# Hybrid decoder trunk: two-tensor work moved from POOL to VectorE, gates split from branch products, a new order of the mixers

## The chip, the cores and the metric

One core of one Trainium2 chip runs the whole program. The time is that of one execution on the device in microseconds, the median of several runs. TensorE (PE) multiplies, VectorE (DVE), ScalarE (ACT) and GpSimd (POOL) work elementwise, SyncE (SP) issues the DMAs. The stationary operand of a matmul comes in by a weight load (PEld), which overlaps the matmul before it.

## What is computed

A decoder trunk of two layers over 512 tokens of width 1024, in float32. In each layer four causal token mixers read one normed input, each is projected, gated and summed; then a feed-forward follows:

```
h = RMSNorm(x)
[u_nsa | u_sb | u_gla | u_fox | gate_logits] = h @ W_in
y_i = mixer_i(u_i)                                       # (512, 512) each
x = x + (sum_i sigmoid(gate_logits_i + b_gate_i) * (y_i @ W_branch_i)) @ W_out
x = x + relu(RMSNorm(x) @ W_ff1)^2 @ W_ff2
```

The mixers are native sparse attention (nsa: 8 heads, of which compressed, selected and sliding-window results are each multiplied by a sigmoid gate and summed), stick-breaking attention (sb), gated linear attention in chunks (gla) and forgetting attention (fox).

## The kernel before, in words

Everything is held transposed: a tile is 128 features x 512 tokens. To keep float32's accuracy at the faster matmul type, each factor is split in a high and a low half (`hh`, `hl` for the input, `wh` and the ring buffer `wr` for the weights, `yh`, `yl` for a mixer's output), and a product takes three matmuls. Weights come as one stream of chunks of 128x1024, 512 KB each, in the very order in which they are used. `chunk` (L305) loads one into a ring of three buffers, ScalarE makes its high half (L315) and VectorE the low half (L316). `mtile` (L319) multiplies a chunk with the input in 24 matmuls of 512 columns; `scaled` (L414) reads the product out of PSUM.

The mixers are cut into pieces, and the list `MIXERS` (L1496) writes out by hand in which order their instructions are issued. `sb_att.1.3` is step 3 of pair of heads 1 of stick-breaking attention, `nsa.2.5` step 5 of pair 2 of nsa, `nsa_cmp.0.1` its compressed part, `gla.0.4` step 4 of pair 0 of gla. The scheduler that builds the program follows the list as a priority and fixes each engine's order at build time by a clock of its own. The same list gives the order of the weight stream (`weight_stream`, L1515).

The places that matter here:
- `branch(n, qt)` (L763) first makes two gates (two `mtile`s, bias, sigmoid; tiles `gt`, two buffers), then multiplies `y_n` by a chunk of `W_branch` (24 matmuls), times the gate on VectorE (L794), added into `mixed` on POOL (L796).
- `nsa(pi)` (L1208): for each head and branch, scores (`pass1`, `pass2`), row maxima, probabilities, `pv`, a reciprocal `r` of the sum; POOL multiplies `r` by the gate row (L1236, 64x512), VectorE by the result (L1238 or L1240), POOL adds the second branch (L1241). `nsa_cmp` adds the compressed part (L1284), and `ysplit` (L748) splits the sum for the branch product.
- `gla(i)` (L1328): VectorE scales `Q` tiles (L1369), the first products use them; later VectorE and ScalarE make the operands of each level (L1392, L1420 to L1425).
- `qk_pair` (L799), `kstack` (L819), `nsa`: casts of a head's rows into `Q1` (L813, L1222) and `B` (L826) on VectorE.
- `rms` (L368) adds squares on VectorE in layer 0 and on POOL in layer 1 (L379); `rope` (L1087) and `gla_gate` (L1325) have one product each on POOL. POOL also does the causal selects (L893, L896, L973) and small copies (L873).

Of the kernel before, what the change touches and what calls it, by code (L numbers as in the profile page):

```python
# [64 lines left out]
class Kern:  # L65
    def __init__(self, tc, A, out, depth, dbg=None):
# [301 lines left out]
    def rms(self, x, bank, early, in_psum=False):  # L368
# [23 lines left out]
        if in_psum:  # L392
            return pb, r
# [62 lines left out]
    def mix(self, l, x):  # L456
# [9 lines left out]
        with self.tc.high_priority(self.tc.cur_priority - p0):  # L466
            self.rb, self.rt = self.rms(x, "d", l == 0)
# [8 lines left out]
        self.mixed, self.begun = None, set()  # L476
# [286 lines left out]
    def branch(self, n, qt):  # L763

        nc = self.nc
        yh, yl = [a for a, _ in self.y[n]], [b for _, b in self.y[n]]
        if qt == 0:
            for i in range(4):
                self.debug(f"y{n}", fb(yh[i][:]), i)
        if self.mixed is None:  # L770
            self.mixed = [self.sb.tile([P, S], F32, name=f"mixed{k}", tag=f"mx{k}", bufs=1) for k in range(KT)]
        gt = []
# [11 lines left out]
        for j in range(2):  # L784
# [10 lines left out]
            if not new:  # L795
                nc.gpsimd.tensor_add(self.mixed[m][:], self.mixed[m][:], g)  # L796


    def qk_pair(self, b_tiles=None):  # L799
# [8 lines left out]
        for b in range(2):  # L808
# [4 lines left out]
            nc.vector.tensor_copy(Q1[ro, :], q32[rr, :])  # L813
# [128 lines left out]
    def sb_att(self, i):  # L942
# [4 lines left out]
        for b in range(2):  # L947
# [61 lines left out]
        self.y.setdefault(1, []).append(self.ysplit(y))  # L1009
# [44 lines left out]
    def fox_qk(self, i):  # L1054
        self.st[3, i] = self.qk_pair(self.B)

    def fox(self, i):
        nc, st, V = self.nc, self.st[3, i], self.vfox
        rr = (slice(0, 64), slice(64, P))
        y = self.dual("yl")  # L1060
        for b in range(2):
# [4 lines left out]
            self.rowmax(S3, Q2[64:96, :], False, nb)  # L1066
            self.pass2(S3, self.B[b], Q2, slice(0, 96))
# [8 lines left out]
        self.y.setdefault(3, []).append(self.ysplit(y))  # L1076


    def rope(self, o, scale, r=None):
# [7 lines left out]
        nc.gpsimd.tensor_mul(s[:], s[:], self.Sn[:])  # L1087
# [120 lines left out]
    def nsa(self, pi):  # L1208
# [3 lines left out]
        if True:  # L1212
            G = [self.gate_rows(pi, 1 + br) for br in range(2)]
            add = self.yn[pi] is not None
            y = self.yn[pi] = self.yn[pi] or self.dual("yl")
            for b in range(2):
                rr = slice(b * 64, b * 64 + 64)
                ro = slice(64 - b * 64, 128 - b * 64)
                qx = q[pi][rr, :]
                Q1, Q2 = self.t("Q1", 512, F32R), self.t("Q2", 512, F32R)  # L1220
                nc.scalar.activation(Q1[rr, :], qx, AF.Copy)
                nc.vector.tensor_copy(Q1[ro, :], qx)  # L1222
                nc.vector.tensor_sub(Q2[0:64, :], qx, fb(Q1[rr, :]))
                for br in range(2):
                    win = br == 1
                    S3 = self.pass1(Ab[2 * br + g], Q1, win)
                    self.rowmax(S3, Q2[64 + 32 * br:96 + 32 * br, :], win)
                    self.pass2(S3, self.B[2 * br + g], Q2, slice(0, 128 if win else 96), win)
# [7 lines left out]
                    nc.gpsimd.tensor_mul(r[rr, :], r[rr, :], G[br][rr, :])  # L1236
                    if br == 0 and not add:
                        nc.vector.tensor_mul(y.f[rr, :], o[od, :], r[rr, :])  # L1238
                    else:
                        nc.vector.tensor_mul(r[rr, :], o[od, :], r[rr, :])  # L1240
                        nc.gpsimd.tensor_add(y.f[rr, :], y.f[rr, :], r[rr, :])  # L1241
                    if not (b and br):
                        yield
        if add:
            self.nsa_done(pi)

    def nsa_done(self, pi):
        self.y.setdefault(0, [None] * 4)[pi] = self.ysplit(self.yn[pi])

    def nsa_cmp(self, g):  # L1250

        nc, q = self.nc, self.q
        sc = self.ps("s")
        self.mm(sc[:], self.KC[g][:, 64:192], q[2 * g][:], True, False)
        self.mm(sc[:], self.KC[g][:, 0:128], q[2 * g + 1][:], False, True)
# [16 lines left out]
        for pi in (2 * g, 2 * g + 1):  # L1272
# [5 lines left out]
            y = self.yn[pi]  # L1278
            if y is None:
# [20 lines left out]

    def gla_b(self, i):
# [4 lines left out]
        if True:  # L1306
            o = self.ps("s")
# [7 lines left out]
            b.append(bb)  # L1315

    def gla_gate(self, j):
# [7 lines left out]
        nc.gpsimd.tensor_mul(g[:], g[:], u[:])  # L1325
        self.gg[j] = g

    def gla(self, i):  # L1328
        nc, l = self.nc, self.l
        q, k, b, V, gate = self.gq, self.gk, self.gb, self.vgla, [self.gg[2 * i], self.gg[2 * i + 1]]  # L1330
        ys = self.y.setdefault(2, [])
        c64 = lambda a: a.rearrange("p (c t) -> p c t", t=64)
        if True:
# [25 lines left out]
            nc.vector.tensor_mul(q64[:], q[i][:], eq[:])  # L1359
# [4 lines left out]
            nc.vector.tensor_mul(k64[:], k[i][:], ek[:])  # L1364
# [27 lines left out]
            nc.vector.tensor_mul(qe[:], qe[:], q[i][:])  # L1392
            nc.vector.tensor_mul(ke[:], ke[:], k[i][:])
# [11 lines left out]
            for li, hf in enumerate(GLA_LEVELS):  # L1405
# [9 lines left out]
                else:  # L1415
# [25 lines left out]
            for hh in range(2):  # L1441
# [22 lines left out]
                ys.append(self.ysplit(y))  # L1464
# [32 lines left out]
sb_qk.0 sb_att.0.0 sb_att.0.1 sb_att.0.2 small_proj sb_qk.1 sb_att.0.3 sb_att.0.4 sb_att.0.5 fox_v.0 sb_att.0.6  # L1497
sb_qk.2 sb_att.0.7 sb_att.1.0 sb_att.1.1 sb_att.1.2 sb_att.1.3 sb_att.1.4 sb_att.2.0 sb_att.1.5 sb_att.2.1
sb_att.1.6 sb_qk.3 sb_att.2.2 nsa_v sb_att.1.7 sb_att.2.3 sb_att.2.4 sb_att.2.5 sb_att.2.6 sb_att.2.7 fox_v.1
fox_qk.0 sb_att.3.0 sb_att.3.1 sb_att.3.2 sb_att.3.3 fox.0.0 sb_att.3.4 fox.0.1 nsa_q.0 fox.0.2 fox_qk.1  # L1500
sb_att.3.5 fox.1.0 sb_att.3.6 sb_att.3.7 nsa_k.1 fox.0.3 branch.1.0 fox.1.1 branch.1.3 fox.1.2 fox_qk.2
branch.1.2 branch.1.1 fox.2.0 fox.2.1 fox.2.2 fox_qk.3 fox.3.0 fox.1.3 cmp_in.0 fox.2.3 fox.3.1 fox.3.2 nsa_k.0
fox.3.3 gla_x.0.0 nsa.0.0 nsa.0.1 nsa_q.1 nsa_q.2 branch.3.1 nsa.0.2 nsa.0.3 nsa.0.4 cmp_in.1 nsa.1.0 branch.3.3
nsa.0.5 nsa.1.1 cmp_step.0.0 cmp_step.1.0 nsa.0.6 nsa_q.3 nsa.1.2 cmp_step.0.1 nsa.0.7 nsa.1.3 branch.3.0
nsa.1.4 nsa.1.5 nsa.1.6 cmp_step.1.1 cmp_step.0.2 cmp_step.1.2 cmp_step.0.3 cmp_step.1.3 branch.3.2 nsa.2.0
cmp_out nsa.1.7 nsa.2.1 nsa.2.2 nsa.2.3 gla_v.0 nsa.2.4 nsa.2.5 nsa_cmp.0.0 nsa.2.6 nsa_cmp.0.1 nsa.2.7
# [3 lines left out]
gla.1.2 gla.1.3 gla.1.4 branch.0.1 gla.1.5 branch.0.0 gla.1.6 gla.1.7 gla.1.8 gla.1.9 gla.1.10 branch.0.3  # L1510
branch.2.1 branch.2.0 branch.2.2 branch.2.3
# [3 lines left out]
def weight_stream(inp, l):  # L1515
# [13 lines left out]
    def branch(n, qt):  # L1529
        for i in range(2):  # L1530
            mt(5936 + n * 1024 + (qt * 2 + i) * P)
        c = qt * 256
        out.append(inp["w_branch"][l][n][:, c:c + 256].reshape(4, P, 256).transpose(1, 0, 2).reshape(P, 1024))

    def qk(q0, k0, i):
# [11 lines left out]
        gla_gate=lambda j: mt(3880 + j * P), branch=branch)  # L1547
# [100 lines left out]
```

## Time and profile before

| | us |
|---|---|
| median of 3 runs | 2240.26 (2240.16 to 2242.59) |
| the profiled execution, device time | 2237.35 |
| its span, first to last instruction | 2235.6 |
| PE busy in the span | 2190.7 (98%) |
| DVE busy | 1640.4 (73%) |
| ACT busy | 1147.3 (51%) |
| POOL busy | 397.6 (18%) |

A span is time in which an engine has an instruction in flight; matmuls overlap, so PE's busy time is not PE at its peak. Layer 0's mixers run to about 725 us, its feed-forward to about 1120; layer 1 repeats both. The mean granted TensorE clock is 0.991 of full speed.

### The profile page before, as it was taken

What the parts mean: (1) busy time and instruction counts of PE and PEld (TensorE: products, weight loads), DVE (VectorE), ACT (ScalarE), POOL (GpSimd) and SP (SyncE); (2) the same over time, 40 slices, a digit from 0 to 9 for tenths busy, and PEclk for the clock granted to TensorE, in tenths of its full rate; (3) what the DMA queues carried; (4) which work ended last, traced back from release to release, by engine and by line L of the source; (5) the groups of instructions that cost most, each with busy time, mean ns of one, the idle gap of its engine ahead of it and who ended that gap; (6) DMA issues with size and microseconds to landing.
All of it is one profiled execution on the core that took longest, in us unless ns stands there. A gap on an engine that the chain in (4) does not pass through costs nothing.

```text
span 2235.6 us, 31530 instructions
## 1 busy us (share of the span) xinstructions
PE 2190.7 (98%) x11888; PEld 1858.1 (83%) x11888; DVE 1640.4 (73%) x2573; ACT 1147.3 (51%) x1777; POOL 397.6 (18%) x741
## 2 busy tenths in 40 slices
PE   8999999999899999999999999999999999999998
PEld 7888878887688898998888888888867888988986
DVE  6889687888975795574558895978788758864655
ACT  5775444434555573453447664444445446543534
POOL 1223024443211000000102230244332110000000
PEclk9999999999899999999999999999999999999999
DMA  4222222322123332322322222223211242323231
GB/s 169 77 67 75 85 75 90 115 91 71 52 79 129 110 107 86 123 90 96 103 94 67 76 76 82 77 93 129 78 66 47 95 152 75 123 72 126 95 104 47
DMA packets 63119, 204.91 MB, mean 92 GB/s; under 512 B 7496, under 2 KB 10184, under 8 KB 62968
## 3 DMA queue, kind: packets, MB, share of 16 engines
q1 hardware_dynamic: 62968, 202.90, 27.4%
q8 instruction: 95, 1.56, 0.3%
q14 instruction: 56, 0.46, 0.1%
HBM read 198.57 MB, written 4.29 MB: 91 GB/s over the span
## 4 chain that ended last, share of the span: by engine, by line
PE 90%; DVE 6%; ACT 1%; issue 1%; DMA 1%; POOL 1%; SPq 0%; DVEq 0%; ACTq 0%; POOLq 0%
PE pd L157 62%; PE ps L157 27%; PE ps L990 1%; DVE Q L876 0%; POOL sm L873 0%; DVE wr1r L316 0%; ACT F L636 0%; DVE sh L1104 0%; DMA wr0f<-in_w 0%; DVE m L1474 0%; DMA x<-in_x 0%; DVE m L379 0%; DMA wr2f<-in_w 0%; DVE m L851 0%; DVE sx L869 0%
## 5 line engine op out<-in xcount | busy, mean ns | idle before, releaser
L157 PE MATMUL pd<-hh,wh 128*128 128x512 f32 x1040 | 415.3, 400 | 0.0
L157 PE MATMUL pd<-hl,wh 128*128 128x512 f32 x1040 | 411.0, 395 | 0.0
L157 PE MATMUL pd<-fx,wh 128*128 128x512 f32 (+1 forms) x1232 | 382.4, 389 | 0.0
L157 PEld LDWEIGHTS pd<-fx,wh 128*128 128x128 f32 x1232 | 230.5, 188 | 47.6
L157 PEld LDWEIGHTS pd<-hh,wh 128*128 128x128 f32 x1040 | 195.6, 188 | 44.1 <-issue 4.0
L157 PEld LDWEIGHTS pd<-hl,wh 128*128 128x128 f32 x1040 | 195.4, 188 | 42.2 <-issue 0.5
L157 PE MATMUL ps<-F,fh 128*128 128x256 f32 x1024 | 194.9, 283 | 1.9 <-ACT p L566 1.9
L157 PEld LDWEIGHTS ps<-F,fh 128*128 128x128 f32 x1024 | 163.5, 191 | 3.2 <-ACT p L566 2.3
L157 PE MATMUL pd<-hh,wr1r 128*128 128x512 f32 x416 | 164.2, 395 | 0.0
L741 DVE TENSOR_TENSOR x<-x,pd 128x512 f32<-128x512 f32 (+1 forms) x63 | 42.7, 678 | 152.3 <-PE pd L157 151.8
L157 PE MATMUL ps<-F,wh 128*128 128x256 f32 x768 | 144.5, 282 | 0.6 <-DVE F L637 0.6
L315 ACT ACTIVATE wh<-wr2f 128x1024 fp32r<-128x1024 f32 x73 | 77.3, 1060 | 122.5 <-PE pd L157 105.6
L315 ACT ACTIVATE wh<-wr0f 128x1024 fp32r<-128x1024 f32 x73 | 77.4, 1060 | 121.0 <-PE pd L157 102.3
L315 ACT ACTIVATE wh<-wr1f 128x1024 fp32r<-128x1024 f32 x72 | 76.2, 1059 | 111.2 <-PE pd L157 85.5
L157 PEld LDWEIGHTS ps<-F,wh 128*128 128x128 f32 x768 | 121.0, 188 | 2.8 <-issue 1.4
L157 PE MATMUL pd<-hh,wr2r 128*128 128x512 f32 x312 | 123.0, 394 | 0.0
L157 PE MATMUL pd<-hh,wr0r 128*128 128x512 f32 x312 | 123.0, 394 | 0.0
L157 PE MATMUL ps<-p,v 128*128 128x384 f32 (+3 forms) x384 | 116.1, 426 | 2.9 <-POOL p L893 2.9
L157 PE MATMUL pd<-yh,wh 128*128 128x512 f32 x256 | 104.8, 409 | 10.0 <-ACT yh L752 9.4
L316 DVE TENSOR_TENSOR wr0r<-wr0f,wh 128x1024 fp32r<-128x1024 f32 x73 | 96.8, 1326 | 19.2 <-ACT wh L315 18.8
L893 POOL TENSOR_SCALAR_AFFINE_SELECT p<-p 128x128 f32<-128x128 f32 x192 | 81.6, 445 | 160.3 <-ACT p L892 158.7
L796 POOL TENSOR_TENSOR mixed<-mixed,gt 128x512 f32<-128x512 f32 x48 | 66.7, 1393 | 243.6 <-DVE gt L794 242.4
(647 smaller groups left out, 5529.5 us busy)
## 6 DMA issues: line engine op xcount, KB each, us to landing
wr0f<-in_w SPq DMA_DIRECT2D x86, 512.0 KB, 3.3
wr2f<-in_w SPq DMA_DIRECT2D x86, 512.0 KB, 3.3
wr1f<-in_w SPq DMA_DIRECT2D x82, 512.0 KB, 3.3
ww3f<-in_w SPq DMA_DIRECT2D x21, 512.0 KB, 3.4
ww7f<-in_w SPq DMA_DIRECT2D x20, 512.0 KB, 3.4
ww5f<-in_w SPq DMA_DIRECT2D x18, 512.0 KB, 3.3
ww8f<-in_w SPq DMA_DIRECT2D x13, 512.0 KB, 4.0
G<-gd SPq DMA_DIRECT2D x48, 128.0 KB, 3.0
```

The lines of the kernel that those rows point to most:

```text
L157: i = self.nc.tensor.matmul(o, l, r, start=start, stop=stop, skip_group_check=True)
L315: nc.scalar.activation(wh[:], raw.f[:], AF.Copy)
L316: nc.vector.tensor_sub(raw[:], raw.f[:], fb(wh[:]))
L741: nc.vector.tensor_add(x[m][:, h], x[m][:, h], o[:, 0:h.stop - h.start])
L796: nc.gpsimd.tensor_add(self.mixed[m][:], self.mixed[m][:], g)
L893: nc.gpsimd.affine_select(d[:, 0:P], d[:, 0:P], [[1, P]], OP.is_gt if strict else OP.is_ge, 0.0, base=0, channel_multiplier=-1)
L990: nc.tensor.transpose(S3[n][:, c:c + P], at(F, q)[:, j * P:(j + 1) * P], self.ident)
```

## The change

1. **No two-tensor operation on POOL** (but for one of 128x4 in `rms`): the adds of `rms`, the adds into `mixed`, and the products of `rope` and `gla_gate` go to VectorE.
2. **nsa's gates once per pair of heads**: the results of both heads stand in new tiles `yw`, one for each branch; after the last step VectorE multiplies each by its gate tile at full height and adds. `G` has four buffers instead of two.
3. **Casts on ScalarE**: the copies into `Q1` and `B`.
4. **Gates are pieces of their own**, `gates.n.qt`, in the list and in the weight stream; `gt` has five buffers instead of two.
5. **A new list `MIXERS`.** Results of mixers are kept by index so that pieces of one kind may come in another order. Assertions tell when a buffer that two mixers share is used out of turn.

The diff, cut to its core:

```diff
-    ATT = (dict(hh=(8, 512), hl=(8, 512), yh=(5, 512), gt=(2, 512), rb=(1, 512)),
+    ATT = (dict(hh=(8, 512), hl=(8, 512), yh=(5, 512), gt=(5, 512), rb=(1, 512)),
...
-                ng=(4, 32), bc=(6, 1), hid=(1, 256), qk=(3, 512), G=(2, 512), smallp=(1, 512), wsm=(1, 256)))
+                ng=(4, 32), bc=(6, 1), hid=(1, 256), qk=(3, 512), G=(4, 512), yw=(2, 512), smallp=(1, 512), wsm=(1, 256)))
...
-        add = nc.vector.tensor_add if early else nc.gpsimd.tensor_add
...
-                add(acc[:], acc[:], sq[:])
+                nc.vector.tensor_add(acc[:], acc[:], sq[:])
...
-    def branch(self, n, qt):
+    def gates(self, n, qt):
...
             self.sigmoid(g[:])
-            gt.append(g)
+            self.gs[n, m] = g
+
+    def branch(self, n, qt):
...
+        gt = [self.gs.pop((n, qt * 2 + i)) for i in range(2)]
         wh, wl = self.chunk()
...
             if not new:
-                nc.gpsimd.tensor_add(self.mixed[m][:], self.mixed[m][:], g)
+                nc.vector.tensor_add(self.mixed[m][:], self.mixed[m][:], g)
...
-            nc.vector.tensor_copy(Q1[ro, :], q32[rr, :])
+            nc.scalar.activation(Q1[ro, :], q32[rr, :], AF.Copy)
...
-            nc.vector.tensor_copy(B[0:64, :], k)
+            nc.scalar.activation(B[0:64, :], k, AF.Copy)
...
-        nc.gpsimd.tensor_mul(s[:], s[:], self.Sn[:])
+        nc.vector.tensor_mul(s[:], s[:], self.Sn[:])
...
+            yb = [self.t("yw") for _ in range(2)]
...
-                nc.vector.tensor_copy(Q1[ro, :], qx)
+                nc.scalar.activation(Q1[ro, :], qx, AF.Copy)
...
-                    nc.gpsimd.tensor_mul(r[rr, :], r[rr, :], G[br][rr, :])
-                    if br == 0 and not add:
-                        nc.vector.tensor_mul(y.f[rr, :], o[od, :], r[rr, :])
-                    else:
-                        nc.vector.tensor_mul(r[rr, :], o[od, :], r[rr, :])
-                        nc.gpsimd.tensor_add(y.f[rr, :], y.f[rr, :], r[rr, :])
+                    nc.vector.tensor_mul(yb[br][rr, :], o[od, :], r[rr, :])
...
+            for br in range(2):
+                nc.vector.tensor_mul(yb[br][:], yb[br][:], G[br][:])
+                if br or add:
+                    nc.vector.tensor_add(y.f[:], (y.f if add else yb[0])[:], yb[br][:])
...
-        nc.gpsimd.tensor_mul(g[:], g[:], u[:])
+        nc.vector.tensor_mul(g[:], g[:], u[:])
...
-nsa_cmp.0.2 gla_b.0 nsa.3.0 gla_gate.0 nsa.3.1 nsa.3.2 nsa.3.3 nsa.3.4 gla_b.1 gla_x.1.0 nsa.3.5 nsa_cmp.1.0
-nsa.3.6 nsa_cmp.1.1 gla_gate.1 gla_v.1 nsa.3.7 nsa_cmp.1.2 gla.0.0 gla_gate.2 gla.0.1 gla.0.2 gla.0.3 gla.0.4
-gla_x.1.1 gla.0.5 gla.0.6 gla.0.7 gla.0.8 gla.0.9 gla_x.0.1 branch.0.2 gla_gate.3 gla.1.0 gla.0.10 gla.1.1
...
+nsa.3.2 gla_b.1 nsa.3.3 nsa.3.4 nsa.3.5 nsa_cmp.0.2 nsa_cmp.1.0 gla_x.1.0 nsa.3.6 gla_gate.1 gla_v.1 nsa_cmp.1.1
+gla.0.0 nsa.3.7 nsa_cmp.1.2 gla.0.1 gla.0.2 gla.0.3 gla_gate.2 gla.0.4 gla.0.5 gla.0.6 gla.0.7 gla_x.1.1 gla.0.8
+gla.0.9 gates.0.0 gla_x.0.1 gates.0.2 gates.0.1 branch.0.2 gla_gate.3 gla.1.0 gla.1.1 gla.0.10 gla.1.2
...
```

## Rows read from the trace of the kernel before

**Rows 1.** The page's first part: busy us, share of the 2235.6 us span, instructions.
```profile
PE 2190.7 (98%) x11888; PEld 1858.1 (83%) x11888; DVE 1640.4 (73%) x2573; ACT 1147.3 (51%) x1777; POOL 397.6 (18%) x741
```
**Rows 2.** Stages: length; PE, PEld, DVE, ACT, POOL busy; clock; DMA share, GB/s.
```profile
300.00:500.00 200.00, 198.76 (x1003) 161.97 (x1002) 164.75 (x333) 86.96 (x154) 78.51 (x160) 1.00 0.29 95
500.00:620.00 120.00, 109.42 (x528) 86.97 (x528) 106.07 (x208) 62.45 (x113) 40.45 (x61) 0.93 0.20 64
...
1600.00:1720.00 120.00, 108.93 (x526) 86.02 (x525) 104.77 (x208) 59.69 (x107) 38.69 (x61) 0.93 0.20 67
```
**Rows 3.** TensorE's waits in 545 to 620 us: us in total, times, longest.
```profile
PE pd L157 <- ACT yh L752: 4.8, 2, 3.1
PE ps L157 <- DVE Q L1369: 3.9, 2, 2.5
```
**Rows 4.** TensorE's timeline: start, us, what, and in brackets the idle time before.
```profile
559.19 0.58 PE L157 MATMUL pd<-yh,wh 128*128 128x512 f32 x1 [1.64 <-ACT yh L752]
...
570.89 0.46 PE L157 MATMUL ps<-Q 64*128 64x128 f32 x2 [2.47 <-DVE Q L1369]
...
579.48 0.79 PE L157 MATMUL pd<-yh,wh 128*128 128x512 f32 x1 [3.12 <-ACT yh L752]
...
587.49 0.39 PE L157 MATMUL pd<-hl,wh 128*128 128x512 f32 x1
587.72 0.39 PE L157 MATMUL pd<-hh,wh 128*128 128x512 f32 x1
```
**Rows 5.** Table by stage again, cut where the granted clock changes.
```profile
559.50:566.30 6.80, 6.17 (x16) 4.54 (x15) 6.74 (x29) 4.24 (x10) 3.42 (x7) 0.50 0.37 120
...
573.10:583.40 10.30, 7.18 (x26) 5.48 (x25) 9.47 (x15) 5.78 (x12) 3.82 (x3) 0.50 0.08 18
```
**Rows 6.** The chain that ended last, in 500 to 620 us: start, us, what.
```profile
575.41 1.68 DVE m L1392
577.09 1.68 DVE yl5f L1284
```
**Rows 7.** POOL's instructions by line: count, busy us, mean ns, idle time before.
```profile
L796 POOL TENSOR_TENSOR mixed<-mixed,gt 128x512 f32<-128x512 f32 x48 | 66.7, 1393 | 243.6 <-DVE gt L794 242.4 <-DVE sm L1181 1.2
...
L1236 POOL TENSOR_TENSOR r<-r,G 64x512 f32<-64x512 f32 x32 | 43.1, 1346 | 87.7 <-issue 76.9 <-ACT r L911 10.2
...
L379 POOL TENSOR_TENSOR m<-m,p 128x512 f32<-128x512 f32 x7 | 11.4, 1635 | 374.7 <-ACT p L378 374.6
```
**Rows 8.** By line in 40 to 300 us (first two) and in 300 to 740 us.
```profile
L316 DVE TENSOR_TENSOR wr2r<-wr2f,wh 128x1024 fp32r<-128x1024 f32 x12 | 14.6, 1214 | 1.7 <-ACT wh L315 1.6
...
L973 POOL TENSOR_SCALAR_AFFINE_SELECT e1f<-e1f 128x128 f32<-128x128 f32 x16 | 9.3, 602 | 9.4 <-ACT e1f L981 5.8 <-DVE e1f L967 3.6
...
L316 DVE TENSOR_TENSOR wr2r<-wr2f,wh 128x1024 fp32r<-128x1024 f32 x18 | 29.8, 1655 | 1.6 <-ACT wh L315 1.6
```
**Rows 9.** VectorE by line over the span; last, durations of L876: min/median/max.
```profile
L316 DVE TENSOR_TENSOR wr2r<-wr2f,wh 128x1024 fp32r<-128x1024 f32 x73 | 96.9, 1327 | 10.6 <-ACT wh L315 10.1
...
L876 DVE TENSOR_TENSOR Q<-cst,sx 32x512 fp32r<-32x512 f32 x48 | 41.0, 854 | 1.5
...
L876 DVE TENSOR_TENSOR Q<-cst,sx x48: 675/684/1808, 180.7 to 1666.3; 32x512 fp32r<-32x512 f32 x48
```
**Rows 10.** Prices, ns min/median/max: a VectorE product, a VectorE cast, a ScalarE copy.
```profile
L794 DVE TENSOR_TENSOR gt<-pd,gt x48: 673/692/693, 350.7 to 1839.3; 128x512 f32<-128x512 f32 x48
...
L813 DVE CAST Q<-qk x32: 420/422/425, 43.0 to 1398.1; 64x512 fp32r<-64x512 f32 x32
...
L812 ACT ACTIVATE Q<-qk x32: 612/628/634, 43.3 to 1396.9; 64x512 fp32r<-64x512 f32 x32
```
**Rows 11.** Busy us in 40 us slices: ScalarE (first), VectorE (the others).
```profile
120.00:160.00 40.00, 31.00 (x69) 1.00 0.21 67
...
540.00:580.00 40.00, 37.68 (x82) 0.83 0.16 53
580.00:620.00 40.00, 36.14 (x71) 0.96 0.20 66
```

More of the change, by code (lines that the diff above doesn't have):

```diff
@@ L365, in vtiles, with rms @@
                 evac(t, acc[t // 2][:, (t % 2) * 256:(t % 2) * 256 + 256])
-    def rms(self, x, bank, early, in_psum=False):
+    def rms(self, x, bank):
         nc = self.nc
         acc = self.t("m")
-        add = nc.vector.tensor_add if early else nc.gpsimd.tensor_add
         for k in range(KT):
@@ L475, in mix @@
         self.dtag = "d"
-        self.mixed, self.begun = None, set()
+        self.mixed, self.begun, self.own, self.gs = None, set(), {}, {}
         self.y, self.Ab, self.st, self.cd, self.gg, self.V = {}, [None] * 4, {}, {}, {}, {}
@@ L779, in branch @@
             self.sigmoid(g[:])
-            gt.append(g)
+            self.gs[n, m] = g
+    def branch(self, n, qt):
+        nc = self.nc
+        yh, yl = ([self.y[n][k][j] for k in range(4)] for j in range(2))
+        if self.mixed is None:
+            self.mixed = [self.sb.tile([P, S], F32, name=f"mixed{k}", tag=f"mx{k}", bufs=1) for k in range(KT)]
+        gt = [self.gs.pop((n, qt * 2 + i)) for i in range(2)]
         wh, wl = self.chunk()
@@ L1024, in fox_v @@
     def fox_v(self, c):
+        self.own["v", c] = 3
         if c == 0:
@@ L1118, in cmp_step @@
         nc, d = self.nc, self.cd[i]
+        self.own["hid", i] = c
         w = self.chunk(False).rearrange("p (l m) -> p l m", l=4)
@@ L1156, in nsa_q @@
         if i == 0:
-            self.q, self.yn = [], [None] * 4
-        self.q.append(self.rope(self.mtile(self.hh, self.hl), 0.125, self.dual("e").f))
+            self.q, self.yn = {}, [None] * 4
+        d = self.dual("e")
+        self.rope(self.mtile(self.hh, self.hl), 0.125, d.f)
+        self.q[i] = d
     def cmp_out(self):
         nc, hid = self.nc, self.hid
+        assert self.own["wsm"] == 0 and self.own["hid", 0] == self.own["hid", 1] == 3
+        self.own["cmp"] = True
         u = self.t("m", 256)
@@ L1278, in nsa_cmp @@
             y = self.yn[pi]
+            assert not self.own.get(("y", pi))
             if y is None:
@@ L1289, in gla_v @@
         self.v_plain("v3", c)
+        self.own["v", c] = 2
         self.vgla = self.V["v3"]
@@ L1306, in gla_b @@
         if True:
+            assert self.own["wsm"] == 1
             o = self.ps("s")
@@ L1501 @@
[L1501 to L1505, printed above, removed]
@@ L1511 @@
-branch.2.1 branch.2.0 branch.2.2 branch.2.3
+sb_qk.0 sb_att.0.0 small_proj sb_qk.1 sb_att.0.1 sb_att.0.2 sb_att.0.3 sb_att.0.4 sb_att.1.0 sb_att.0.5 sb_qk.2
+sb_att.0.6 sb_att.1.1 sb_att.1.2 fox_v.0 sb_att.0.7 sb_att.1.3 sb_att.1.4 sb_att.2.0 sb_qk.3 sb_att.1.5
+sb_att.2.1 sb_att.1.6 sb_att.1.7 sb_att.2.2 sb_att.2.3 nsa_v sb_att.2.4 sb_att.2.5 fox_qk.0 sb_att.3.0
+sb_att.3.1 sb_att.2.6 sb_att.3.2 fox_v.1 fox.0.0 sb_att.2.7 sb_att.3.3 sb_att.3.4 sb_att.3.5 sb_att.3.6 nsa_q.0
+fox.0.1 fox.0.2 fox_qk.1 fox.1.0 sb_att.3.7 gates.1.3 fox.0.3 gates.1.0 branch.1.0 fox.1.1 nsa_k.1 fox.1.2
@@ new lines @@
+branch.1.3 fox_qk.2 gates.1.2 branch.1.2 gates.1.1 branch.1.1 fox.2.0 fox.2.1 fox.2.2 fox_qk.3 cmp_in.0 fox.1.3
+fox.2.3 fox.3.0 fox.3.1 fox.3.2 nsa_k.0 gla_x.0.0 nsa_q.1 fox.3.3 nsa.0.0 gates.3.1 branch.3.1 nsa_q.3 nsa.0.1
+nsa.0.2 gates.3.3 nsa.0.3 cmp_in.1 nsa.0.4 nsa.0.5 nsa.1.0 nsa.0.6 nsa.1.1 branch.3.3 nsa_q.2 cmp_step.1.0
+nsa.1.2 nsa.0.7 nsa.1.3 gates.3.0 branch.3.0 nsa.1.4 nsa.1.5 cmp_step.1.1 cmp_step.0.0 nsa.1.6 cmp_step.0.1
+cmp_step.1.2 cmp_step.0.2 cmp_step.0.3 cmp_step.1.3 gates.3.2 branch.3.2 nsa.1.7 nsa.2.0 cmp_out nsa.2.1 nsa.2.2
@@ new lines @@
+gla_v.0 nsa.2.3 nsa.2.4 nsa_cmp.0.0 nsa.2.5 nsa.2.6 nsa_cmp.0.1 nsa.3.0 gla_b.0 nsa.2.7 gla_gate.0 nsa.3.1
+nsa.3.2 gla_b.1 nsa.3.3 nsa.3.4 nsa.3.5 nsa_cmp.0.2 nsa_cmp.1.0 gla_x.1.0 nsa.3.6 gla_gate.1 gla_v.1 nsa_cmp.1.1
+gla.0.0 nsa.3.7 nsa_cmp.1.2 gla.0.1 gla.0.2 gla.0.3 gla_gate.2 gla.0.4 gla.0.5 gla.0.6 gla.0.7 gla_x.1.1 gla.0.8
+gla.0.9 gates.0.0 gla_x.0.1 gates.0.2 gates.0.1 branch.0.2 gla_gate.3 gla.1.0 gla.1.1 gla.0.10 gla.1.2
+branch.0.1 gla.1.3 gla.1.4 gla.1.5 gla.1.6 gla.1.7 gla.1.8 gates.0.3 gla.1.9 gla.1.10 branch.0.0 gates.2.1
@@ L1512 @@
+branch.0.3 gates.2.2 branch.2.1 gates.2.3 branch.2.3 gates.2.0 branch.2.0 branch.2.2
 """.split()]
@@ L1527, in weight_stream, with gates, branch @@
         z[i] = inp[f"nsa_cmp_w{n}1"][l].reshape(16, P, 256).transpose(1, 0, 2)
-    def branch(n, qt):
+    def gates(n, qt):
         for i in range(2):
             mt(5936 + n * 1024 + (qt * 2 + i) * P)
+    def branch(n, qt):
         c = qt * 256
@@ L1546, in weight_stream @@
         gla_v=lambda c: vt(r(3352 + c * 256, 256)), gla_x=lambda n, i: mt((2840, 3096)[n] + i * P),
-        gla_gate=lambda j: mt(3880 + j * P), branch=branch)
+        gla_gate=lambda j: mt(3880 + j * P), gates=gates, branch=branch)
     for c in range(2):
```

78 lines of the change are left out of this document (37 added, 41 removed).

## Prediction

> **What bounds the kernel now.** Read in this order. First the busy line: TensorE has matmuls in flight for 2190.7 of 2235.6 us [rows 1], so nothing that leaves its work alone can give more than 45 us, and the change leaves it alone: the same matmuls of the same shapes, in another order. The number to look for is therefore where TensorE stands idle. Second, the table by stage. In 300 to 500 us it idles 1.24 us; in 500 to 620 us 10.58, and in the second layer's twin, 1600 to 1720, 11.07 [rows 2]. These two stretches, in which nsa ends and gla begins, hold 21.7 of the 45 us; most of the rest is the start, the end and the feed-forward, which the change doesn't touch. Third, who ended these waits: in 545 to 620 us the high half of a mixer's output, `yh` (4.8 us), and the factors `Q` that gla scales at L1369 (3.9 us) [rows 3]. The timeline puts them in three places, 559, 571 and 579 us [rows 4]. Fourth, the clock: right after the first wait and after the 2.47 us wait the granted clock is 0.50, the lower level, for 6.8 and 10.3 us, and in the next row of the table it would be 1.00 again [rows 5]. So the idle time is paid twice.
>
> **Why these waits exist.** The chain before 579 us runs through VectorE: L1392 took 1.68 us, and then L1284, the last sum into nsa's output, another 1.68 [rows 6]. A clean two-tensor VectorE operation of 128x512 takes 0.69 us (L794) [rows 10]. Both run while POOL works on a two-tensor operation (L1241, then L1325). The same is seen at large on the weight split L316: 1.214 us where POOL has only selects and small copies (40 to 300 us), 1.655 where it also has two-tensor operations [rows 8]. The order of TensorE's work is fixed when the program is built. There it reaches a branch product of nsa, `branch.0.2`, before gla's first products; nsa's output is not ready, and everything behind it waits [rows 3, 4].
>
> **The change, part by part.**
>
> *POOL to VectorE.* POOL has 123 two-tensor operations on large tiles: 48 adds into `mixed` at 1.39 us, 32 gate products of nsa at 1.35, 16 adds of nsa, 12 in `rope`, 8 in `gla_gate`, 7 in `rms` of layer 1 at 1.64 (three of the six kinds stand in [rows 7]). VectorE gets 48 + 12 + 8 + 7 of them as they are. For nsa, a pair of heads had 4 half-height products and 2 half-height adds on POOL, and gets 2 full products and 1 full add: 8 pairs in two layers, 24 operations. That is 99 x 0.69 = **+68 us** of VectorE time [rows 10].
>
> *VectorE to ScalarE.* 72 casts of 64x512 leave VectorE, 48 into `Q1` (L813, L1222) and 24 into `B` (L826), all of one form, at the 0.42 us of L813: **-30 us**. On ScalarE they cost 0.63 each, +45 us [rows 10]. Its fullest stretch is 31.0 of 40 us [rows 11]; two `sb_qk` there add four copies, 2.5 us, and cover remains. If ScalarE had been the limit there, the 45 us would count; at 78% I cost them at nothing.
>
> *What VectorE stops losing.* Lower bound from rows that stand: the 73 splits through `wr2r` average 1.327 against 1.214 clean, 8.2 us; those through `wr0r` the same; L876 0.854 against its median of 0.684, 48 times, 8.2: 25 us [rows 8, 9]. Upper bound: each of the 123 holds one VectorE operation for about 1 us, 123 us. I take half of them, **-62 us**: in the stretch of rows 8, the 18 `wr2r` splits lost 7.9 us together, so about 8 of 18 were caught. Sum for VectorE: 68 - 30 - 62 = -24 us, between +13 and -85. VectorE is thus not relieved much; its operations only last what they last alone.
>
> By the Trainium skill, "SBUF — State Buffer", section "Who interferes with whom", a VectorE operation with two SBUF inputs and a POOL operation that reads SBUF lock each other out, whichever comes first. By that rule the 99 moved operations would collide with POOL's remaining selects and copies. The trace agrees only for one side: in 40 to 300 us the selects L973 stretch to 0.602 us, the splits don't [rows 8].
>
> *Gates apart from branch products, and the new order.* A gate's product needs only `hh`, `hl` and a weight chunk; a branch product needs a mixer's finished output. In the old list the pieces behind `gla.0.9` that need no mixer are `gla_x.0.1` and the two gates inside `branch.0.2`: 3 chunks of 24 matmuls. In the new list `gates.0.0 gla_x.0.1 gates.0.2 gates.0.1` stand there, 7 chunks, before the first branch product. At 0.23 us from start to start (the last two rows of [rows 4]), 5.5 us for 24 matmuls, that is 38 us of work that can be put in front of a wait, where there were 16. Five `gt` buffers instead of two let the results stand. Moving whole gates moves their weight transfers on the SP queue as well; the list sets the stream's order, so none is passed by another. Bound of this edit: nothing, or all of the 4.8 us that `yh` costs in each layer. I take all of it, since 38 us exceed the 22 us from 557 to 579 [rows 4].
>
> *gla's own waits* (3.9 us in each layer, Q L1369) end after VectorE operations of which some were held up. Bounds 0 and 3.9; I take half, 2.0, because VectorE stays full there: 37.68 and 36.14 of 40 us [rows 11]. The remaining idle time of the stretch (10.58 - 4.8 - 3.9 = 1.9 us) I leave.
>
> *The clock.* TensorE is busy for 6.17 + 7.18 = 13.35 us at 0.50 in layer 0, with a like pair in layer 1 [rows 5]. At full clock that work takes half: 6.7 us in each layer. Bounds 0 and 13.4 for both. By the Trainium skill, "TensorE: Matmul & The Clock Gate", Part 1, activity holds the clock up and idleness lets it drop; by that all 13.4 would come back, and without it nothing. Each fall here comes just behind an idle stretch of over 1.6 us [rows 4, 5], two of three of which go, so I take the 13.4.
>
> *Smaller edits.* In `rms` of layer 1 seven adds stand on VectorE instead of POOL at the layer's border, beside products that need no `rb`: nothing, or 7 x 0.69 = 4.8 us if VectorE is late there. `G` loads may go out earlier (four buffers): nothing. Separate buffers `yw` free a PSUM bank without the gate product's 1.35 us: counted under the waits.
>
> **Sum.** Per layer 4.8 + 2.0 + 6.7 = 13.5; both layers 27. From the profiled execution, 2237.35 us (a span of 2235.6 and 1.75 around it), 2210.4. That execution stands 2.9 below the median of 2240.26; from the median: **2213 us**.
>
> **Rivals.** (1) *Only the branch waits go.* VectorE remains the limit in 540 to 620 us, gla's waits and the second fall of the clock stay: 2 x (4.8 + 6.17/2) = 16 us less some new waits, 2226. For it: VectorE's 92% there. Against: two operations of its chain there lost 1 us each to POOL [rows 6, 10]. (2) *All goes*, with the 2 us idle in 300 to 500 and its twin: 21.7 + 13.4 + 2 = 37, 2203. (3) *The waits move.* The list is new everywhere, and a static order that is right by its builder's clock may put another unready product in front: no net change, 2239. Here belongs too that contention only changes sides, selects waiting on VectorE instead; POOL's 82% idle speaks against it. (4) *Slower: gates bring their VectorE work along.* Each chunk costs VectorE 1.21 for the split, 0.69 for the scaling and about 0.5 for the bias. Four gates more than before inside 540 to 620 us are 9.6 us on an engine with 73.8 of 80 us taken. From the point where that need exceeds the stretch, TensorE waits for splits and for gla's operands alike, the clock falls as before, and up to 9.6 us a layer are lost; half of it gives 2250.
>
> **How the numbers follow.** Forecast 2213: 0.45. Rival 1, 2226: 0.23. Rival 2, 2203: 0.12. Rival 3, 2239: 0.10. Rival 4, 2250: 0.10. A measurement of this kernel tells about 0.2%, 4.5 us, from no change. Faster: 0.45 + 0.23 + 0.12 = 0.80; the same 0.10; slower 0.10. The range from 2198 to 2240 takes in all but rival 4 and half of rival 3; the low end is rival 2 with VectorE's loss at its upper bound.
>
> **What would show it.** Right: VectorE's L316 near 1.22 us everywhere; no POOL two-tensor operation beyond `rt`; gate products between gla's first pieces; the clock at 1.00 through both stretches; idle time there under 5 us. Wrong: a new entry over 3 us among TensorE's waits, a clock at 0.50 elsewhere, or VectorE above 95% in a 40 us slice with TensorE waiting for L316.

## The result and the profile after

The changed kernel takes **2210.66 us** (median; 2209.95 to 2210.93) against 2240.21 for the kernel before: a ratio of 0.987, 95% interval 0.9858 to 0.9882, 29.5 us less. The forecast was 2213. The profiled execution has a span of 2208.9 us, 26.7 less than before's. All that follows compares profiles with profiles and medians with medians.

The busy line of the page after, to be held against [rows 1]:

```profile
PE 2180.6 (99%) x11888; PEld 1850.7 (84%) x11888; DVE 1605.5 (73%) x2600; ACT 1193.9 (54%) x1849; POOL 214.8 (10%) x618
```

VectorE lost 34.9 us though it has 27 instructions more, ScalarE gained 46.6, POOL lost 182.8. Table by stage after (length; PE, PEld, DVE, ACT, POOL busy; clock; DMA share, GB/s), against [rows 2]:

```profile
0.00:40.00 40.00, 31.69 (x208) 30.28 (x209) 25.09 (x49) 22.06 (x34) 6.30 (x20) 0.91 0.54 184
...
300.00:500.00 200.00, 200.00 (x1020) 164.69 (x1019) 162.18 (x351) 96.39 (x167) 40.24 (x132) 1.00 0.29 95
500.00:620.00 120.00, 117.28 (x587) 92.77 (x586) 107.18 (x224) 71.32 (x126) 16.76 (x46) 1.00 0.20 67
...
1600.00:1720.00 120.00, 117.28 (x581) 92.46 (x581) 106.46 (x222) 70.30 (x123) 14.15 (x36) 1.00 0.20 67
```

TensorE's idle time in the two stretches where nsa ends and gla begins fell from 21.65 to 5.44 us, and the clock is at its upper level through both. The two pieces of [rows 5] that ran at 0.50 are now full and at 1.00; the lower level turns up in a new place, 18.2 to 25.0 us, at the start:

```profile
559.50:566.30 6.80, 6.80 (x33) 5.65 (x32) 6.80 (x23) 3.67 (x9) 2.58 (x6) 1.00 0.24 81
573.10:583.40 10.30, 10.30 (x66) 8.68 (x63) 10.07 (x20) 6.75 (x13) 1.05 (x2) 1.00 0.14 52
...
18.20:25.00 6.80, 6.80 (x33) 6.80 (x33) 4.89 (x10) 0.00 (x0) 1.02 (x1) 0.50 0.19 56
```

The five largest of TensorE's waits over the whole span (us in total, times, longest). Those of [rows 3], for `yh` and for gla's `Q` of L1369 (L1389 after), are gone from the whole list; the waits for gla's level factors `G` and for `Q` of L1460 are new:

```profile
PE ps L157 <- ACT hh L405: 6.8, 1, 6.8
PE ps L157 <- DVE G L1445: 3.7, 2, 1.8
PE pd L157 <- DVE r L443: 3.1, 1, 3.1
PE ps L157 <- ACT p L563: 1.9, 2, 1.0
PE ps L157 <- DVE Q L1460: 1.8, 2, 0.9
```

TensorE's timeline shows the new order (start, us, what, idle before), against [rows 4]. Input products (`hh`, `hl`) fill the time to 588 us, with gla's first products between them; only then does the first branch product (`yh`) start, which began at 556 us before:

```profile
587.80 0.39 PE L157 MATMUL pd<-hl,wh 128*128 128x512 f32 x1
588.03 0.39 PE L157 MATMUL pd<-yh,wh 128*128 128x512 f32 x1
...
593.67 1.13 PE L157 MATMUL ps<-G,p 128*128 128x128 f32 x8 [1.84 <-DVE G L1445]
...
599.08 0.71 PE L157 MATMUL ps<-Q,v 128*128 128x128 f32 x4 [0.88 <-DVE Q L1460]
```

ScalarE's copies that make the two `yh` that TensorE waited for at 559 and 579 us, first before, then after:

```profile
558.51 0.63 ACT L752 ACTIVATE yh<-yl4f 128x512 fp32r<-128x512 f32 x1
...
578.80 0.63 ACT L752 ACTIVATE yh<-yl5f 128x512 fp32r<-128x512 f32 x1 [2.34 <-DVE yl5f L1284]
```

```profile
555.32 0.63 ACT L749 ACTIVATE yh<-yl4f 128x512 fp32r<-128x512 f32 x1
...
578.68 0.64 ACT L749 ACTIVATE yh<-yl5f 128x512 fp32r<-128x512 f32 x1
```

The first comes 3.2 us sooner, the second 0.1. So the longer of the two waits (3.12 us) went because TensorE asks later, not because VectorE delivers sooner.

Last, the groups by line: the split L316 has one duration now, against 1.327 in [rows 9], and POOL's one two-tensor line is that of `rt`:

```profile
L316 DVE TENSOR_TENSOR wr0r<-wr0f,wh 128x1024 fp32r<-128x1024 f32 x74 | 90.5, 1223 | 19.3 <-ACT wh L315 19.0
L316 DVE TENSOR_TENSOR wr2r<-wr2f,wh 128x1024 fp32r<-128x1024 f32 x74 | 90.4, 1222 | 12.2 <-ACT wh L315 12.0
...
L384 POOL TENSOR_TENSOR rt<-rt,mhalf 128x4 f32<-128x4 f32 x2 | 2.0, 1020 | 51.3 <-DVE rt L383 51.3
```

**The balance.** TensorE's idle time over the whole span fell from 44.9 to 28.3 us: -16.6, of which -16.2 in the two stretches. Its busy time fell from 2190.7 to 2180.6 us: -10.1. That is the clock: the work at half clock in the two stretches, 13.35 us in the first layer and 13.72 in the second, takes half (-13.5), and the start's 6.80 us at half clock cost +3.4. Together -26.7 us, by which the span fell.

### The profile page after: what moved, and what is told of

It is laid out like the page before. It is cut to its first block, busy times and chain, and to the rows that moved or that the text cites. A ratio compares the mean times of both kernels' runs of the same rounds, so it can differ in the third digit from the quotient of the medians.

```text
span 2208.9 us, 31398 instructions
## 1 busy us (share of the span) xinstructions
PE 2180.6 (99%) x11888; PEld 1850.7 (84%) x11888; DVE 1605.5 (73%) x2600; ACT 1193.9 (54%) x1849; POOL 214.8 (10%) x618
## 4 chain that ended last, share of the span: by engine, by line
PE 93%; DVE 4%; ACT 1%; issue 1%; DMA 0%; POOL 0%; SPq 0%; DVEq 0%; ACTq 0%
PE pd L157 64%; PE ps L157 28%; PE ps L990 1%; DVE Q L1460 0%; DVE p L1443 0%; DVE G L1445 0%; ACT F L633 0%; ACT hh L405 0%; DVE p L1439 0%; ACT wh L592 0%; DMA x<-in_x 0%; ACT wh L315 0%; DVE p L449 0%; DVE p L1440 0%; DVE wr1r L316 0%
## 5 line engine op out<-in xcount | busy, mean ns | idle before, releaser
L157 PE MATMUL pd<-hh,wr1r 128*128 128x512 f32 x384 | 153.2, 399 | 0.0
L157 PE MATMUL pd<-hh,wr2r 128*128 128x512 f32 x328 | 129.2, 394 | 0.0
L157 PE MATMUL pd<-hh,wr0r 128*128 128x512 f32 x328 | 129.2, 394 | 0.0
L316 DVE TENSOR_TENSOR wr0r<-wr0f,wh 128x1024 fp32r<-128x1024 f32 x74 | 90.5, 1223 | 19.3 <-ACT wh L315 19.0
L316 DVE TENSOR_TENSOR wr2r<-wr2f,wh 128x1024 fp32r<-128x1024 f32 x74 | 90.4, 1222 | 12.2 <-ACT wh L315 12.0
```

Of the source, the lines that this page charges most:

```text
L157: i = self.nc.tensor.matmul(o, l, r, start=start, stop=stop, skip_group_check=True)
L316: nc.vector.tensor_sub(raw[:], raw.f[:], fb(wh[:]))
```

## Experiments

Two theories stood first. **A, contention:** the gain comes from VectorE, whose operations POOL no longer holds up. **B, the list:** it comes from products that need no mixer, put in front of the waits. Below, "held up" is a sum worked out from a trace: of each VectorE instruction that lasted over 100 ns longer than is usual for its line and shape while POOL worked, the excess. Before it is 61 us beside POOL's two-tensor lines; after it is under 2 in all. Each ratio is to the kernel before, run beside it on the same chip; after's is 0.9870.

### The operations and the list, one without the other

**e3: the list without the operations.** The changed kernel with before's arithmetic: POOL's two-tensor work and VectorE's casts as they were, the new `MIXERS`, gates apart.

```diff
-                nc.vector.tensor_add(self.mixed[m][:], self.mixed[m][:], g)
+                nc.gpsimd.tensor_add(self.mixed[m][:], self.mixed[m][:], g)
...
-            nc.scalar.activation(Q1[ro, :], q32[rr, :], AF.Copy)
+            nc.vector.tensor_copy(Q1[ro, :], q32[rr, :])
```

> The new list and the gates apart alone: POOL has its two-tensor operations, VectorE its casts, nsa its products once per head. Theory A: 2230 us or more. Theory B: 2218 us or less. Against e1_pool_back it also tells the casts: if ScalarE's relief of VectorE counts, this one is over 3 us slower than e1_pool_back.

Measured: 2229.85, ratio 0.9963 (0.9951 to 0.9976). The list (with the gates apart and the larger buffers) is worth 8 us by itself, over a quarter of the gain.

**e1: POOL's work back, the rest of the change kept** (casts on ScalarE, new list).

> The changed kernel with its new list and its gates apart, but the adds into mixed, the products of rope, gla_gate and nsa (once per head again) and the adds of rms in layer 1 back on POOL; the casts stay on ScalarE. Theory A, the gain comes from VectorE operations that POOL no longer holds up: L316 in 300 to 740 us rises again above 1.35 us on average, TensorE idles over 8 us in 500 to 620 us, the clock falls to 0.50 once, 2228 us or more. Theory B, the gain comes from the list, which puts products that need no mixer into the gap: VectorE loses its 50 to 60 us again, but the products cover it, 2216 us or less. Between the two both count; I hold 2221 for likeliest.

Measured: 2223.91, 0.9934 (0.9919 to 0.9949). VectorE's busy time is 1603.4, after's within 2 us, because what it is spared it loses again: 58 us held up. All waits of TensorE in 545 to 620 us, one row that is the same, to the digit, in e1 and e3:

```profile
PE ps L157 <- DVE G L1444: 4.4, 2, 3.6
```

After waits 1.8 us for the same `G`. So POOL's two-tensor work has a price under the new list, 14 us by the ratios (0.9934 - 0.9870), but half of the gain stays without its removal. How much of the 14 is holding up, and how much POOL's longer operations inside nsa's own chain, this run doesn't tell. Against e3, which differs by the casts alone, it also gives the casts a price of 6 us while POOL's work is in place.

**e2: all operations of the change, the old list** (gates stand straight before their branch).

```diff
-gla.0.9 gates.0.0 gla_x.0.1 gates.0.2 gates.0.1 branch.0.2 gla_gate.3 gla.1.0 gla.1.1 gla.0.10 gla.1.2
+gla_x.1.1 gla.0.5 gla.0.6 gla.0.7 gla.0.8 gla.0.9 gla_x.0.1 gates.0.2 branch.0.2 gla_gate.3 gla.1.0 gla.0.10 gla.1.1
```

> The changed kernel with the old list: each gates piece stands straight before its branch piece, where it was before; all operations as in the changed kernel. Theory A (POOL's holding up is the cause): the branch product of nsa may still come early, but its input is ready sooner; 2220 us or less, idle time in 500 to 620 us under 6 us. Theory B (the list is the cause): the branch product still waits for yh at about 557 and 579 us, half clock follows, 2232 us or more.

Measured: 2282.04, 1.0195 (1.0179 to 1.021): **43 us slower than before**, with nothing held up any more and VectorE at 1604.8. This fells theory A as a sufficient cause. TensorE's timeline, the longer waits:

```profile
575.22 2.08 PE L157 MATMUL ps<-m,VC 64*128 64x512 f32 x4 [6.78 <-DVE m L1287]
579.95 0.80 PE L157 MATMUL pd<-yh,wh 128*128 128x512 f32 x1 [2.65 <-ACT yh L749]
...
591.01 0.60 PE L157 MATMUL ps<-Q 64*128 64x128 f32 x2 [4.03 <-DVE Q L1389]
...
598.81 0.80 PE L157 MATMUL pd<-yh,wh 128*128 128x512 f32 x1 [3.07 <-ACT yh L749]
```

The first wait stands nowhere before: `nsa_cmp` needs its transposed probabilities (L1287), the end of some ten VectorE operations, and the old list has one step of nsa between `nsa_cmp.1.0`, which makes them, and `nsa_cmp.1.1`, which needs them. In the new list `gla_x.1.0`, `gla_gate.1` and `gla_v.1`, products of the input, stand between the two as well. Behind the wait `yh` and `Q` are late as before.

**e10: the new list with each gate glued to its branch** (the changed kernel otherwise; only the places of the `gates` pieces differ, throughout the list). The lines around `branch.0.2`:

```diff
-gla.0.9 gates.0.0 gla_x.0.1 gates.0.2 gates.0.1 branch.0.2 gla_gate.3 gla.1.0 gla.1.1 gla.0.10 gla.1.2
+gla.0.4 gla.0.5 gla.0.6 gla.0.7 gla_x.1.1 gla.0.8 gla.0.9 gla_x.0.1 gates.0.2 branch.0.2 gla_gate.3 gla.1.0 gla.1.1
```

> The changed kernel with its new list, but each gates piece straight before its branch piece: the order of everything else as in the changed kernel. Theory of the free products: of the seven chunks behind gla.0.9 three remain, TensorE waits again for yh or for gla's operands near 560 to 590 us, the clock falls, 2222 to 2240. If the rest of the list does it: within 4 us of 2211.

Measured: 2235.85, 0.9987 (0.9978 to 0.9997). One stage, and the two largest waits in 545 to 620 us:

```profile
500.00:620.00 120.00, 110.14 (x558) 87.70 (x557) 104.29 (x224) 66.11 (x118) 17.74 (x47) 0.97 0.19 62
```

```profile
PE ps L157 <- DVE Q L1389: 5.9, 2, 5.7
PE ps L157 <- DVE G L1445: 2.8, 2, 1.8
```

26 us of the gain are gone by the ratios. Idle time in this stage is at 9.86 us, near before's 10.58, and the clock falls again: the gain rests on where the gates stand (13.2 of the 17.9 us by which idle time grows against after lie in the two stretches). What they cover is not what the prediction named, though. `yh` is waited for 0.3 us in the whole span; the idle time stands in front of gla's `Q`:

```profile
560.61 0.39 PE L157 MATMUL pd<-yh,wh 128*128 128x512 f32 x1
...
573.42 0.77 PE L157 MATMUL ps<-Q 64*128 64x128 f32 x2 [5.65 <-DVE Q L1389]
...
581.08 0.47 PE L157 MATMUL pd<-yh,wh 128*128 128x512 f32 x1
```

The branch product begins without a wait behind three chunks, and its last `yh`, made at 577.85 us here, is asked for only behind the wait for `Q`. What time TensorE loses in front of `Q` it can't lose again in front of the `yh` behind it, so the two waits are not two separate prices. And the gain rests on the gates together with the operations, as e3 shows. So B alone falls too, and a third theory is formed, **C, the pair**: an order that is fixed at build time fits one set of durations; operations and list have to be changed together.

### Contention by itself

**e4 and e9: ghosts.** The changed kernel with 100 POOL operations more, at the places where POOL's old ones stood, into a scratch tile that nothing reads; in e4 products of two inputs, in e9 copies of one. To make room, two small tiles have fewer buffers (`ng` 1, `sm` 4).

```diff
+                self.ghost(self.mixed[m][:], g)
...
+    def ghost(self, a, b, rr=slice(0, P)):
+        self.nc.gpsimd.tensor_mul(self.t("gh", 448, BF16)[rr, :], a[:, 0:448], b[:, 0:448])   # e4
+        self.nc.gpsimd.tensor_copy(self.t("gh", 448, BF16)[rr, :], a[:, 0:448])               # e9
```

> The changed kernel with 100 POOL two-tensor operations added whose results nobody reads: beside each add into mixed, each reciprocal of nsa, each rope and each gla_gate one product of 448 columns of the same inputs into a scratch tile (two small buffers made smaller to fit it). No chain passes through POOL, so only the holding up of VectorE comes back. If that is what cost time: VectorE's busy time rises by 30 us or more and the time by 5 to 15 us, 2216 to 2226. If it was the 1.3 us that each step of a chain took on POOL: VectorE's time rises as much, the kernel's by under 3 us. If POOL is held up rather than VectorE: VectorE's busy time stays within 10 us of 1605.

> The ghost kernel with each of the 100 added POOL operations turned from a two-input product into a one-input copy of the same tile, same places, same scratch tile, same two smaller buffers. If POOL's two-input reads hold VectorE up and cost the 29 us of the ghost kernel: VectorE's busy time falls back to within 8 us of 1605 and the time to 2208 to 2218. If it is only that POOL reads and is full, or that the added reads keep buffers longer or changed the order: 2228 to 2242.

Measured: e4 2240.11, 1.0003 (0.9994 to 1.0012), VectorE 1635.3; e9 2232.82, 0.9970 (0.9957 to 0.9983), VectorE 1611.8. Products held VectorE up by 31.9 us in 46 operations, copies by 6.9 in 24. One meeting of each kind, with the same VectorE operation, 0.69 us by its median, e4 first:

```profile
349.46 1.14 POOL L799 TENSOR_TENSOR gh<-mixed,gt 128x448 bf16<-128x448 f32 x1 [1.80 <-DVE mixed L794]
349.50 1.65 DVE L794 TENSOR_TENSOR mixed<-mixed,gt 128x512 f32<-128x512 f32 x1
```

```profile
348.02 0.56 POOL L799 CAST gh<-mixed 128x448 bf16<-128x448 f32 x1 [2.30 <-DVE mixed L794]
348.08 1.05 DVE L794 TENSOR_TENSOR mixed<-mixed,gt 128x512 f32<-128x512 f32 x1
```

VectorE's operation ends 0.55 us after POOL's in both. The copy holds it up as the product does, only for a shorter time. So it is over both traces: of VectorE's operations with two inputs in SBUF that start while a ghost runs, 43 of 55 in e4 and 20 of 27 in e9 are held up, nearly all by what POOL's operation has left less some 0.14 us; of those that start before the ghost, none (of 31 and 34).

In time, e4 and e9 are 7 us apart (0.0033), for 23.5 us of VectorE's. That is not a clean price of holding up, since e4's products also keep a second source (`gt`, `G`) longer. The other 22 us (0.9970 - 0.9870) are hardly contention: the copies cost them with 6.9 us held up. They may come from sources that are held longer (`mixed`, `r`), from the fewer buffers, or from the order, which is built anew with them; this was not taken apart.

### Each edit alone, under the old list

Four kernels start from the one before. e5: POOL's work in `mixed`, `rope`, `gla_gate` and `rms` to VectorE. e6: the casts to ScalarE. e7: nsa's gates once per pair. e8: only the buffers, `gt` 5 and `G` 4.

```diff
-    ATT = (dict(hh=(8, 512), hl=(8, 512), yh=(5, 512), gt=(2, 512), rb=(1, 512)),
+    ATT = (dict(hh=(8, 512), hl=(8, 512), yh=(5, 512), gt=(5, 512), rb=(1, 512)),
```

> The kernel before with one edit: the adds into mixed and of rms and the products of rope and gla_gate go from POOL to VectorE. Old list, old buffers. E2 (all edits but the list) took 2282, so something in it costs 43 us. Theory C, an order fixed at build time fits only the operations it was sought with, and any edit under the old list opens waits: 2245 to 2265 here. Theory D, the five gt buffers do it, since gates and their branch product are then placed earlier: here within 6 us of 2239. If the edit by itself were a gain, as VectorE's sum of -24 us says: 2225 to 2235.

> The kernel before with one edit: the 72 casts go to ScalarE. Old list. Theory C: 2243 or more, with new TensorE waits. Theory D: 2230 to 2242, VectorE's 30 us less shows as a gain or as nothing. e1 against e3 (the same edit under the new list) gave -6.

> The kernel before with one edit: nsa's gate once per pair of heads on VectorE (yw tiles, two G buffers as before). Old list. Theory C: 2245 to 2265, since y of a pair is now ready only after its last step while the list still asks for it early. Theory D: 2230 to 2242.

> The kernel before with five gt and four G buffers, nothing else. Theory D: 2260 or more, the branch product of nsa placed still earlier and TensorE waiting for yh over 8 us in each layer. Theory C: 2235 to 2250, a small part of E2's 43 us.

| | us | ratio (95%) | VectorE busy |
|---|---|---|---|
| e5 moves | 2243.75 | 1.0024 (1.0014 to 1.0033) | 1645.9 |
| e6 casts | 2271.98 | 1.0152 (1.0132 to 1.0172) | 1599.3 |
| e7 nsa | 2259.82 | 1.0090 (1.0069 to 1.0111) | 1624.8 |
| e8 buffers | 2251.58 | 1.0058 (1.0041 to 1.0075) | 1636.1 |

Every one is slower than the kernel before, e6 the most although it takes 41 us off VectorE. In e6 and e8 the waits for `yh` grow, from 9.4 us over the span to 19.4 and 25.0. e8 shows it most plainly, its arithmetic being before's; TensorE's timeline:

```profile
565.58 0.80 PE L157 MATMUL pd<-yh,wh 128*128 128x512 f32 x1 [5.99 <-ACT yh L752]
...
574.98 0.46 PE L157 MATMUL ps<-Q 64*128 64x128 f32 x2 [2.69 <-DVE Q L1369]
...
584.94 0.80 PE L157 MATMUL pd<-yh,wh 128*128 128x512 f32 x1 [5.23 <-ACT yh L752]
```

With more `gt` buffers a gate doesn't wait for an older one to be used. That the gates went out earlier and left less in front of the branch is the likely reading; it was not isolated. The buffers are then 13 of e2's 43 us: theory D of the expectations is not enough, and e6 and e7 lose without them. e7 has the 6.78 us wait for nsa's compressed part that e2 has:

```profile
565.39 2.08 PE L157 MATMUL ps<-m,VC 64*128 64x512 f32 x4 [6.78 <-DVE m L1272]
```

### Two edits on the changed kernel

**e11: the casts back on VectorE,** all else as changed.

> The changed kernel with the 72 casts on VectorE again. VectorE 30 us busier, ScalarE 45 us less. If VectorE is still near its limit under the new list: 2214 to 2222. If the casts cost nothing where they are: within 2 us of 2211.

Measured: 2230.54, 0.9962 (0.9949 to 0.9975); VectorE 1630.4, ScalarE 1150.4. The casts, which cost 34 us under the old list (e6), are worth 21 under the new one. The time is that of e3 (0.9963), in which POOL's two-tensor work is back as well and VectorE is held up again: with the casts on VectorE, taking that work off POOL gains nothing. The prices of the edits don't add up, under the new list either. TensorE's waits in 500 to 620 us:

```profile
PE ps L157 <- DVE G L1445: 5.4, 2, 3.8
PE pd L157 <- DVE yl5r L750: 0.7, 1, 0.7
```

**e12: VectorE relieved further.** The gate's bias goes into ScalarE's first exponential; the clamp at -44 is left out. 64 VectorE operations go, two small ones that negate the bias come.

```diff
-            nc.vector.tensor_scalar(g[:], g[:], self.sp(self.l, C_BG + n * 8 + m), -44.0, OP.add, OP.max)
-            self.sigmoid(g[:])
+            self.sigmoid(g[:], self.nbg[:, n * 8 + m:n * 8 + m + 1])
```

> The changed kernel with 64 VectorE operations fewer: a gate's bias goes into ScalarE's first Exp as a per-partition bias, negated once per layer, and the clamp at -44 falls away. VectorE 31 us less. If VectorE is what still ends TensorE's waits (5.5 us before gla's products at 594 us and its twin): 2203 to 2209. If the new list fits only the operations it was made for: 2212 to 2230.

Measured: 2215.20, 0.9891 (0.9876 to 0.9905), which overlaps after's interval: no gain. The stage that was to profit did:

```profile
500.00:620.00 120.00, 118.92 (x599) 94.20 (x598) 106.39 (x222) 71.93 (x127) 16.19 (x46) 1.00 0.21 71
```

Its idle time falls from 2.72 to 1.08 us, as in the second layer, and VectorE has 1579.1 in all; but 300 to 500 us, full in the changed kernel, has 1.22 us idle again. There is little idle time left for such an edit to remove. The span is 5.1 us longer although TensorE idles less in it (26.6 us against 28.3): its busy time is longer, 2187.4 against 2180.6, at a clock that is no lower (0.997 against 0.996). Why was not found.

## Why the prediction was right, point by point

- **What bounds the kernel:** right. The gain is TensorE's idle time and half clock in the two stretches. None of the time came from TensorE doing less. The bound of 45 us is wrong, though: it counts idle time alone, and of the 26.7 us gained 10.1 are busy time, by the clock.
- **Waits for `yh`, 4.8 us a layer, all taken:** the size is right, 9.4 to 0, and so is that the order did most of it: the second `yh` is made 0.1 us earlier than before, and the branch starts 32 us later. That the gates were needed for it is not shown: glued (e10) they leave 0.3 us of waiting for `yh`, and what comes back is the wait for `Q`.
- **gla's waits, half of 3.9 us a layer:** about right, for another reason than a relieved VectorE. With the gates glued, gla waits 5.9 us for its first factors (e10), though VectorE is as relieved as after (1604.4 us busy): it is the order that takes this wait away. After, it is gone whole; in its place gla waits 1.84 us for `G` and 0.88 for `Q` further on, 2.7 a layer instead of 1.95. The 1.9 us a layer that the sum left standing went too.
- **The clock, 13.4 us:** right for the two stretches, but not as argued: the second fall stood behind the wait for `Q` at 571 us, of which the sum left half, so by its own terms not all of the 13.4 had to come back. Waits of like length went both ways: after the 1.84 us for `G` the clock stays at 1.00, where before 0.50 came behind 1.64 us. The start was overlooked: the clock is at 0.50 from 18.2 to 25.0 us, where it was 1.00. It is a term that the sum lacked, some 3.4 us.
- **VectorE, -24 us, of it -62 held up:** the size was good, -34.9 in all and 60 held up. What failed is the step from it to time, which the prediction left unpriced ("VectorE is thus not relieved much; its operations only last what they last alone"). e2 has the same relief and is 43 us slower than before; e6 has more of it and is 34 slower; under the new list the casts' 25 us are worth 21 (e11). A microsecond of VectorE has no price of its own here: it counts where TensorE's fixed order waits for it.
- **Casts on ScalarE at nothing:** right on ScalarE's side. It gained 46.6 us of the 45 expected, and 120 to 160 us, its fullest stretch, has 33.66 us busy of 40 while TensorE is busy for all 40.00.
- **The buffers at nothing:** wrong by themselves, the old list loses 13 us with the buffers alone (e8); under the new list no run leaves them out. Adding terms, each costed against the profile of before, came out right with an order that fits all of them; under the old list the same operations and buffers lose 43 us (e2).
- **The rule on locks:** By the Trainium skill, "SBUF — State Buffer", section "Who interferes with whom", the moved operations would meet POOL's selects and copies. The traces agree, in kind: after, a split L316 lasts up to 1.32 us beside a select, against 1.22 by its median, and e9's copies hold VectorE up until they end. So the prediction's reading that the splits don't stretch beside selects holds for its 260 us alone. The effect is small, under 2 us in all, where these operations are short, 0.3 us for most selects.
- **Rivals:** Rival 4, gates bringing VectorE work, did not come: 540 to 580 us has VectorE at 38.29 of 40 us and TensorE at 40.00. Rival 3, an order that puts an unready product in front, came in small, with `G`, and is what the same operations do under the old list (e2); so it was the right one to fear.
- **The signs that were named:** those of being right came: L316 at 1.22 us, no two-tensor operation on POOL but `rt`, gate products between gla's first pieces, the clock at 1.00 in both stretches, and idle time of 2.72 us in each. Two of the three signs of being wrong came as well: a new entry over 3 us among the waits (`G`, 3.7 in both layers together) and a clock at 0.50 elsewhere (the start). Neither was large enough to undo the gain.
- **The number:** the sum of -27 met the profiled executions, 2237.35 and 2210.59, with -26.8. That it is so close is in part luck: idle time fell by 3.0 us more than the sum's 13.6 (4.8 + 2.0 in each layer), and the start, which the sum lacked, cost 3.4. The 2.3 us between 2213 and 2210.66 is the distance of before's profile to its median, 2.9, which after's doesn't have.

**What stays open:** why exactly each edit lengthens the waits under the old list (only e2's and e7's compressed part was followed in the trace); the 22 us of e9 that are hardly contention; e12's longer busy time; and the half clock at the start. The first 40 us have a mean of 0.91 in after, e2, e10 and e11, 0.96 in e1, e3, e4, e7, e8 and e12, 1.00 in before, e5, e6 and e9: it goes with no single edit. Each of these is one execution.

## What to carry to other kernels

Where an engine's order is fixed when the program is built, an edit is worth what it is worth together with that order: four edits that each lose under the old list win together under the new one, so seek the order again before an edit is dropped. Look in the profile for work that needs nothing of the late result (here gates, 5.5 us each 24 matmuls), put it in front of the wait, and see whether the next product behind it is ready; idle time of the bottleneck engine was paid twice, in waiting and in the clock behind it. Relieving a busy engine that is not the bottleneck moved the time by anything between 21 us less (the casts under the new list) and 34 more (the same casts under the old), so ask which wait ends on it, not how busy it is.

## What the runs showed of the hardware

A VectorE operation with two inputs in SBUF that starts while POOL runs an operation on SBUF is lengthened by about what POOL has left, whether POOL reads two inputs or one: by 0.96 us with 1.11 us of a product left (e4), by 0.36 with 0.50 of a copy left (e9), by 0.12 with 0.26 of a select left (after). If VectorE's starts first, it is not held up (none of 31 in e4, of 34 in e9). Shorter work on POOL costs VectorE less: 100 products of up to 128x448 cost 31.9 us, 100 copies of the same shape 6.9; at their shortest a product took 1.13 us, a copy 0.55.

The clock's lower level can come up with next to no change in the idle time: the first 18.2 us have 9.89 us of TensorE busy after and 10.13 before, and only after is followed by 6.8 us at 0.50.
